# A pool of 46 slots in place of 45, and the modulation steps' unread products in a slot

## The chip, the core and the metric

The kernel runs on one core of one Trainium2 chip. The metric is the device time of one execution in microseconds (us). Engines are named as the profile names them: PE is TensorE (matmuls), PEld its loads of the stationary operand, DVE is VectorE, ACT is ScalarE, POOL is GpSimd, SP issues nearly all DMAs. SBUF is the on-chip memory of 128 partitions in which all tiles below lie, PSUM the accumulators of TensorE.

## What is computed

Two layers of a diffusion backbone on 640 tokens (512 latent, 128 context) of width 1024. A layer is an FFN, a mixer and a second FFN, each with a residual, a norm and a modulation of its own:

```
mod = silu(cond) @ ada_w + ada_b          # per layer: sh1, sc1, g1, sh2, sc2, g2, sh3, sc3, g3
h = rmsnorm(x, p['norm'][0]) * (1 + sc1) + sh1
x = x + 0.5 * g1 * swiglu(h, p['wg'][0], p['wu'][0], p['wd'][0])
h = rmsnorm(x, p['norm'][1]) * (1 + sc2) + sh2
x = x + g2 * mixer(h)                     # window means | attention | order-2 Hyena, then w_out
h = rmsnorm(x, p['norm'][2]) * (1 + sc3) + sh3
x = x + 0.5 * g3 * swiglu(h, p['wg'][1], p['wu'][1], p['wd'][1])
```

with `swiglu(h) = (silu(h @ wg) * (h @ wu)) @ wd` and an inner width of 2816. The context's attention keys and values are outputs too.

## The kernel before, in words

**Arithmetic.** Tokens are columns, features are partitions; `x` stays in SBUF as 8 chunks of 128 features by 640 tokens, worked on in two halves of 320 (`HT`). Each fp32 operand is split into a high and a low part (`hhi`, `hlo` for activations, `whi`, `wlo` for weights: ScalarE casts, L295, VectorE subtracts, L296), and three matmuls stand for one. Most gate and up products of an FFN go through `Seven`, a scheme that makes seven block products of eight.

**An FFN** (`ffn`, L684 and following) has 22 inner chunks in three parts of 8, 7 and 7. For each part it makes the inner chunks (`pr`, then its split `ahi`, `alo`) and then adds their part of the down projection to `x` for the 8 output chunks (`residual`, L566 to L572). In the last part the first three output chunks are made with weights loaded as they come; the last five (`DNSKEW`), the *tail*, have their weights kept in SBUF (`load_keep`, L312: tiles `kwh`, `kwl`) and are done half by half: all five for half 0, then all five for half 1, so that the next norm of half 0 can start while half 1 is multiplied. After each chunk `ssq_add` (L451) squares the new `x` on ScalarE (L453) and adds it to the sum on VectorE (L455), both into a slot `sq`. `Norm.stat` (L472) sums these over features with a matmul (`tot`, L477), makes `var` (L480) and `rs` on POOL; `scale` makes `dg` (L499), `apply` makes `y`, `hhi`, `hlo`.

**The pool of slots** (`sp`, L213) has `SLOTS` tiles of 640 fp32 numbers per partition under one tag. Nearly everything that lives longer than a moment takes one through `slot` or `slot3`: `hhi`, `hlo`, `pr`, `ahi`, `alo`, `y`, `sq`, `kwh`, `kwl`, the twisted inputs of `Seven`, the mixer's tables and spectra. A new tile has to wait until one of the pool's tiles is free.

**The modulation.** Three of the nine groups of layer 0 are made on TensorE in the prologue. The other 15 (of both layers) are made in steps on VectorE: a step multiplies a 128 by 1024 tile of `ada_w` (`araw`) by the conditioning vector and sums along the row into one column of `mods`; the instruction also writes the 1024 products, which nothing reads (`junk`, L408 to L411). A DMA of 512 KB (L401) serves two steps, and two `araw` tiles take turns. There are 240 steps, 80 each in the first FFN of layer 0, the second FFN of layer 0 and the first FFN of layer 1 (`PLAN`); none in the mixers or the last FFN. `ada_plan` spreads them over an FFN by weights (`ADAW`), and `ada_tick` issues those that are due: after each inner chunk (following `pack`), after each output chunk, and in the tail after each chunk of half 0. `issue_after` holds a step behind the last residual or `pr` product.

**What sets the order.** Each engine's instructions are put in order when the kernel is built: by their place in the program's text, by the priorities that `tc.high_priority` gives to weight loads and splits, and by when their inputs and tiles are free. TensorE's order is the text's. The order of the text in the tail matters here:

```
for d in range(DC - tail):                            # chunks 0, 1, 2
    if tail and d == DC - tail - 1:
        kept.append(load_keep(src(d + 1)))            # chunk 3's weights
    ...residual and ssq_add for both halves...
    ada_tick(last_w if end else down_w)               # L781
...
kept += [load_keep(src(d)) for d in ds_[len(kept):]]  # L786: chunks 4 to 7
nxt.kept = nxt.lead()                                 # first weights of the next stage
for half in range(2):
    for q, d in enumerate(ds_):
        residual(...); ssq_add(d, half)
        if half == 0: ada_tick(tail_w)                # L793
        if half == 1 and q == ST: nxt.stat(0)
```

Of the kernel before, what the change touches and what calls it, by code (L numbers as in the profile page):

```python
# [13 lines left out]
BF16 = mybir.dt.bfloat16  # L14
# [3 lines left out]
P = 128  # L18
# [14 lines left out]
PROT = 8  # L33
AG0 = (1, 0, 2)
MIXT = 70
SLOTS = 45
PF = 8
WB = 5
EXB = 7
# [144 lines left out]
def hybrid_kernel(ctx: ExitStack, tc: tile.TileContext, a, depth=2, fc=22):  # L184
# [27 lines left out]
    wp = ctx.enter_context(tc.tile_pool(name="wp", bufs=4))  # L212
    sp = ctx.enter_context(tc.tile_pool(name="sp", bufs=SLOTS))  # L213
    tp = ctx.enter_context(tc.tile_pool(name="tp", bufs=2))
# [8 lines left out]
    def nm(s):  # L223
        count[0] += 1
        return f"{s}{count[0]}"

    def slot(n=NCOL, dt=F32, name="s"):
        return sp.tile([P, n], dt, tag="s", name=nm(name))
# [7 lines left out]
    def tiny(n, name="t", bufs=4):  # L236
        return tp.tile([P, n], F32, tag=f"{name}{n}", bufs=bufs, name=nm(name))
# [4 lines left out]
    def mix(n=512, name="mx"):  # L242
        return acc(n, mx, name)
# [130 lines left out]
    def bias(l, g):  # L374
        return PR(l, "adab").rearrange("p (g s c r) -> p g s c r", g=9, s=2, c=4)[:, g]
# [21 lines left out]
    def ada_group(l, g):  # L397

        def load(n):
            raw = wp.tile([P, 1024], F32, tag="araw", bufs=ARAWB, name=nm("araw"))  # L400
            DMA.dma_start(out=raw, in_=a["adat"][l * 9 + g - len(AG0), n])  # L401
            ada_raw[l, g, n] = raw

        def step(n):
            raw = ada_raw[l, g, n // 2]
            i, r = n // 2, n % 2
            c, s = i // 2, i % 2
            junk = tp.tile([P, 1024], BF16, tag="junk", bufs=1, name=nm("junk"))  # L408
            with tc.issue_after(pace[0]) if pace else nullcontext():
                V.tensor_tensor_reduce(out=junk, in0=raw, in1=condb[:, r], scale=1.0, scalar=bias(l, g)[:, s, c, r:r + 1],  # L410
                                       op0=ALU.mult, op1=ALU.add, accum_out=mods[l][:, g, c, s, r:r + 1])  # L411
            if n == 2 * DC - 1:
                done.add((l, g))

        for n in range(2 * DC):
            ada_q.append(((lambda n=n: load(n // 2)) if n % 2 == 0 else None, lambda n=n: step(n)))
# [41 lines left out]
    class Norm:  # L458
# [13 lines left out]
        def stat(self, half):  # L472
            if self.key[::3] in done:
                self.affine()
            s = ssq[half]
            tot = mix(3, "tot")
            for t, o in enumerate((0, P, HT - P)):  # L477
                PE.matmul(out=tot[:, t:t + 1], lhsT=s[:, o:o + P], rhs=ones[:, 0:1], start=True, stop=True)
            var = tiny(3, "var")
            V.tensor_scalar(out=var, in0=tot, scalar1=1.0 / 1024.0, scalar2=EPS, op0=ALU.mult, op1=ALU.add)  # L480
            rs = tiny(3, "rs")
            G.tensor_tensor(out=rs, in0=var, in1=mhalf, op=ALU.pow)
            self.rs = rs
# [1327 lines left out]
```

## Time and profile before

| | us |
|---|---|
| median of three executions | 2406.22 |
| the three executions | 2406.14, 2406.22, 2408.6 |
| the profiled execution | 2408.28 |
| span in its trace | 2406.5 |
| PE busy | 2363.9 (98%) |
| PEld busy | 2240.9 (93%) |
| DVE busy | 1919.6 (80%) |
| ACT busy | 1094.1 (45%) |

The profiled execution's time is its span and 1.8 us around it. The busy share of an engine is an average over stages. In this kernel the first FFN of layer 0 reaches from about 100 to 545 us, its mixer to 825, its second FFN to 1258, and layer 1 follows the same pattern, its first FFN to 1695 and its mixer to 1973. PEclk in a table of windows is the granted clock of TensorE as a share of full speed. A matmul's record of 0.31 us overlaps the next; starts come 0.15 us apart when nothing is waited for. In a timeline, a row with xN stands for N instructions in a row, and the idle time before it stands in brackets with what ended it; a start that lies a little before the end of the instruction ahead is overlap.

### The profile page before, as it was taken

What the parts mean: (1) busy time and instruction counts of PE and PEld (TensorE: products, weight loads), DVE (VectorE), ACT (ScalarE), POOL (GpSimd) and SP (SyncE); (2) the same over time, 40 slices, a digit from 0 to 9 for tenths busy, and PEclk for the clock granted to TensorE, in tenths of its full rate; (3) what the DMA queues carried; (4) which work ended last, traced back from release to release, by engine and by line L of the source; (5) the groups of instructions that cost most, each with busy time, mean ns of one, the idle gap of its engine ahead of it and who ended that gap; (6) DMA issues with size and microseconds to landing.
All of it is one profiled execution on the core that took longest, in us unless ns stands there. A gap on an engine that the chain in (4) does not pass through costs nothing.

```text
span 2406.5 us, 41068 instructions
## 1 busy us (share of the span) xinstructions
PE 2363.9 (98%) x15576; PEld 2240.9 (93%) x15576; DVE 1919.6 (80%) x3885; ACT 1094.1 (45%) x2228; POOL 18.2 (1%) x46
## 2 busy tenths in 40 slices
PE   8999999999989999999999999999998999999999
PEld 3799999999877999999999999999987799999999
DVE  7888888996786798888989889898778678567583
ACT  4654352534345553453535435253434555335251
POOL 0000000000000000000000000000000000000000
PEclk9999999999989999999999999999999999999999
DMA  9434434353310235344343343534231022222222
GB/s 320 173 101 128 134 117 155 107 172 114 102 45 14 71 110 162 124 125 144 115 137 108 119 136 115 166 110 158 91 112 54 18 71 80 79 84 78 85 68 90
DMA packets 132646, 270.37 MB, mean 112 GB/s; under 512 B 15002, under 2 KB 24924, under 8 KB 132320
## 3 DMA queue, kind: packets, MB, share of 16 engines
q1 hardware_dynamic: 132448, 267.75, 34.8%
q8 instruction: 122, 2.00, 0.4%
q14 instruction: 76, 0.62, 0.1%
HBM read 259.56 MB, written 8.13 MB: 111 GB/s over the span
## 4 chain that ended last, share of the span: by engine, by line
PE 88%; DVE 6%; issue 2%; DMA 1%; ACT 1%; SPq 1%; POOL 0%; POOLq 0%; DVEq 0%; ACTq 0%
PE mm L205 74%; PE Z L205 5%; PE yt L205 1%; PE o L205 1%; PE pt L209 1%; DVE junk L410 1%; PE fk L205 1%; PE mx L205 1%; PE ada L205 1%; PE zf L205 1%; DVE kwl L296 0%; DMA kf<-store 0%; DVE wlo L296 0%; PE rsb L205 0%; DVE rp L1308 0%
## 5 line engine op out<-in xcount | busy, mean ns | idle before, releaser
L205 PE MATMUL mm<-hhi,whi 128*128 128x320 f32 x1440 | 448.4, 311 | 1.1 <-ACT u L1224 1.1
L295 ACT CAST whi<-raw 128x512 fp32r<-128x512 f32 (+1 forms) x394 | 238.7, 606 | 463.3 <-PE mm L205 423.0
L205 PE MATMUL mm<-hlo,whi 128*128 128x320 f32 x1440 | 446.3, 310 | 0.0
L205 PE MATMUL mm<-hhi,wlo 128*128 128x320 f32 x1440 | 446.0, 310 | 0.0
L205 PE MATMUL mm<-alo,whi 128*128 128x320 f32 x1198 | 370.8, 310 | 0.8 <-DVE alo L296 0.8
L205 PE MATMUL mm<-ahi,whi 128*128 128x320 f32 x1198 | 370.8, 310 | 0.0
L205 PE MATMUL mm<-ahi,wlo 128*128 128x320 f32 x1198 | 370.7, 309 | 0.0
L296 DVE TENSOR_TENSOR wlo<-raw,whi 128x512 fp32r<-128x512 f32 (+1 forms) x394 | 263.3, 671 | 75.7 <-ACT whi L295 71.3
L410 DVE CUSTOM_DVE_ANT_0 junk<-araw,condb,par 128x1024 bf16<-128x1024 f32 x240 | 307.4, 1281 | 2.1 <-DMA araw<-in_adat 0.8
L205 PEld LDWEIGHTS mm<-hhi,whi 128*128 128x128 f32 x1440 | 270.5, 188 | 5.9 <-ACT u L1224 2.8
L205 PEld LDWEIGHTS mm<-hlo,whi 128*128 128x128 f32 x1440 | 270.8, 188 | 1.9 <-issue 1.8
L205 PEld LDWEIGHTS mm<-hhi,wlo 128*128 128x128 f32 x1440 | 270.5, 188 | 1.4 <-issue 1.4
L205 PE MATMUL mm<-tlo,whi 128*128 128x320 f32 x864 | 267.4, 309 | 0.0
L205 PE MATMUL mm<-thi,whi 128*128 128x320 f32 x864 | 267.4, 309 | 0.0
L205 PE MATMUL mm<-thi,wlo 128*128 128x320 f32 x864 | 267.3, 309 | 0.0
L205 PEld LDWEIGHTS mm<-alo,whi 128*128 128x128 f32 x1198 | 225.0, 188 | 1.0 <-DVE alo L296 1.0
L205 PEld LDWEIGHTS mm<-ahi,whi 128*128 128x128 f32 x1198 | 225.0, 188 | 0.1
L205 PEld LDWEIGHTS mm<-ahi,wlo 128*128 128x128 f32 x1198 | 225.0, 188 | 0.0
L295 ACT CAST whi<-ex 128x512 fp32r<-128x512 f32 x216 | 134.2, 621 | 188.0 <-PE mm L205 175.6
L296 DVE TENSOR_TENSOR wlo<-ex,whi 128x512 fp32r<-128x512 f32 x216 | 149.2, 691 | 32.6 <-ACT whi L295 28.4
L295 ACT CAST whi<-ws 128x512 fp32r<-128x512 f32 x144 | 89.4, 621 | 162.2 <-PE mm L205 123.1
L205 PEld LDWEIGHTS mm<-thi,whi 128*128 128x128 f32 x864 | 162.3, 188 | 0.0
(263 smaller groups left out, 4704.2 us busy)
## 6 DMA issues: line engine op xcount, KB each, us to landing
araw<-in_adat SPq DMA_DIRECT2D x120, 512.0 KB, 3.6
raw<-in_wgu SPq DMA_DIRECT2D x208, 256.0 KB, 3.1
ex<-in_wgu SPq DMA_DIRECT2D x144, 256.0 KB, 2.7
raw<-in_wd SPq DMA_DIRECT2D x128, 256.0 KB, 2.7
raw<-in_win SPq DMA_DIRECT2D x56, 256.0 KB, 3.0
ar<-in_ada SPq DMA_DIRECT2D x48, 256.0 KB, 5.4
raw<-in_wd SPq DMA_DIRECT2D x64, 192.0 KB, 2.6
tab<-in_tfi SPq DMA_DIRECT2D x32, 256.0 KB, 3.9
```

Source lines behind the costliest of these rows:

```text
L205: cls.order(nc.tensor.matmul(**k))
L209: cls.order(nc.tensor.transpose(**k))
L295: S.copy(out=hi, in_=src)
L296: V.tensor_tensor(out=lo, in0=src, in1=hi.bitcast(F32), op=ALU.subtract)
L410: V.tensor_tensor_reduce(out=junk, in0=raw, in1=condb[:, r], scale=1.0, scalar=bias(l, g)[:, s, c, r:r + 1], op0=ALU.mult, op1=ALU.add, ac ...
```

## The change

The pool has one tile more. The products that nothing reads go to a slot of that pool instead of to a tile of their own (128 partitions by 1024 bf16 numbers, one buffer, from the pool `tp`). `var`, three numbers per partition, has two buffers in place of four. Nothing else is changed.

```diff
--- before.py
+++ after.py
@@ -33,7 +33,7 @@
 PROT = 8
 AG0 = (1, 0, 2)
 MIXT = 70
-SLOTS = 45
+SLOTS = 46
 PF = 8
 WB = 5
 EXB = 7
@@ -405,7 +405,7 @@
             raw = ada_raw[l, g, n // 2]
             i, r = n // 2, n % 2
             c, s = i // 2, i % 2
-            junk = tp.tile([P, 1024], BF16, tag="junk", bufs=1, name=nm("junk"))
+            junk = slot(1024, BF16, "junk")
             with tc.issue_after(pace[0]) if pace else nullcontext():
                 V.tensor_tensor_reduce(out=junk, in0=raw, in1=condb[:, r], scale=1.0, scalar=bias(l, g)[:, s, c, r:r + 1],
                                        op0=ALU.mult, op1=ALU.add, accum_out=mods[l][:, g, c, s, r:r + 1])
@@ -476,7 +476,7 @@
             tot = mix(3, "tot")
             for t, o in enumerate((0, P, HT - P)):
                 PE.matmul(out=tot[:, t:t + 1], lhsT=s[:, o:o + P], rhs=ones[:, 0:1], start=True, stop=True)
-            var = tiny(3, "var")
+            var = tiny(3, "var", 2)
             V.tensor_scalar(out=var, in0=tot, scalar1=1.0 / 1024.0, scalar2=EPS, op0=ALU.mult, op1=ALU.add)
             rs = tiny(3, "rs")
             G.tensor_tensor(out=rs, in0=var, in1=mhalf, op=ALU.pow)
```

## Rows read from the trace of the kernel before

**Rows 1.** Page, part 1: busy us (share of the span) x instructions, per engine
```profile
PE 2363.9 (98%) x15576; PEld 2240.9 (93%) x15576; DVE 1919.6 (80%) x3885; ACT 1094.1 (45%) x2228; POOL 18.2 (1%) x46
```

**Rows 2.** Windows by stage: length, busy sum, PE, PEld, DVE, ACT, POOL, PEclk, DMA share, GB/s
```profile
120.00:480.00 360.00, 360.00 (x2457) 360.00 (x2456) 309.73 (x553) 160.38 (x303) 1.07 (x3) 1.00 0.40 124
510.00:540.00 30.00, 28.93 (x198) 28.41 (x197) 27.82 (x61) 10.45 (x21) 0.85 (x1) 1.00 0.63 205
...
650.00:710.00 60.00, 50.14 (x277) 42.99 (x277) 49.44 (x129) 27.92 (x69) 0.56 (x8) 0.93 0.22 76
```

**Rows 3.** Waits of TensorE: us in total, times, longest us
```profile
PE yt L205 <- DVE wlo L296: 8.3, 2, 4.2
PE pt L209 <- DVE sc L1357: 7.6, 4, 3.6
...
PE tot L205 <- DVE sq L455: 1.0, 1, 1.0
```

**Rows 4.** Page, part 5: the modulation steps; busy us, mean ns | idle before
```profile
L410 DVE CUSTOM_DVE_ANT_0 junk<-araw,condb,par 128x1024 bf16<-128x1024 f32 x240 | 307.4, 1281 | 2.1 <-DMA araw<-in_adat 0.8
```

**Rows 5.** Timeline of VectorE, first FFN's tail: start, us, engine, line, op [idle <-releaser]
```profile
511.18 0.34 DVE L572 SCALAR_TENSOR_TENSOR x<-mm,g,x 128x128 f32<-128x128 f32 x1
511.43 1.28 DVE L410 CUSTOM_DVE_ANT_0 junk<-araw,condb,par 128x1024 bf16<-128x1024 f32 x1
...
512.63 1.16 DVE L296 TENSOR_TENSOR kwl<-raw,kwh 128x512 fp32r<-128x512 f32 x2
...
515.18 1.28 DVE L410 CUSTOM_DVE_ANT_0 junk<-araw,condb,par 128x1024 bf16<-128x1024 f32 x1
...
516.38 0.55 DVE L566 SCALAR_TENSOR_TENSOR x<-mm,g,x 128x320 f32<-128x320 f32 x1
516.85 1.28 DVE L410 CUSTOM_DVE_ANT_0 junk<-araw,condb,par 128x1024 bf16<-128x1024 f32 x1
...
519.12 1.28 DVE L410 CUSTOM_DVE_ANT_0 junk<-araw,condb,par 128x1024 bf16<-128x1024 f32 x1
...
521.86 1.28 DVE L410 CUSTOM_DVE_ANT_0 junk<-araw,condb,par 128x1024 bf16<-128x1024 f32 x1
...
526.34 1.28 DVE L410 CUSTOM_DVE_ANT_0 junk<-araw,condb,par 128x1024 bf16<-128x1024 f32 x1
...
528.61 0.69 DVE L296 TENSOR_TENSOR kwl<-raw,kwh 128x512 fp32r<-128x512 f32 x1
...
534.88 0.50 DVE L455 TENSOR_TENSOR sq<-sq,sq 128x320 f32<-128x320 f32 x1
```

**Rows 6.** Timeline of ScalarE, the same tail
```profile
524.02 2.69 ACT L295 CAST kwh<-raw 128x512 fp32r<-128x512 f32 x4 [4.64 <-DMA raw<-in_win]
526.61 0.47 ACT L453 ACTIVATE sq<-x 128x320 f32<-128x320 f32 x1
```

**Rows 7.** Timeline of TensorE, the same tail
```profile
512.97 0.31 PE L205 MATMUL mm<-alo,kwh 128*128 128x320 f32 x1
513.38 0.41 PE L205 MATMUL mm<-ahi,kwl 128*128 128x320 f32 x1
```

**Rows 8.** Timeline of SP's DMA queue, the same tail
```profile
508.89 4.18 SPq L401 DMA_DIRECT2D araw<-in_adat  x2
```

**Rows 9.** Page, part 6, DMA issues: count, KB each, us to landing
```profile
araw<-in_adat SPq DMA_DIRECT2D x120, 512.0 KB, 3.6
```

**Rows 10.** Timeline of VectorE, second FFN's tail
```profile
1235.60 1.28 DVE L410 CUSTOM_DVE_ANT_0 junk<-araw,condb,par 128x1024 bf16<-128x1024 f32 x1
```

**Rows 11.** Timeline of SP's DMA queue, first mixer
```profile
677.24 1.75 SPq L261 DMA_DIRECT2D tab<-in_tfi  x4
```

**Rows 12.** Windows, first mixer; columns as in rows 2
```profile
676.00:680.00 4.00, 0.00 (x0) 0.00 (x0) 4.00 (x13) 0.58 (x1) 0.00 (x0) 1.00 0.40 130
```

**Rows 13.** Windows, after a wait in the first mixer; columns as in rows 2
```profile
708.00:716.00 8.00, 6.62 (x17) 4.23 (x17) 8.00 (x20) 5.24 (x11) 0.00 (x0) 0.57 0.10 33
```

## The prediction, made before the changed kernel was run

> **What bounds the kernel now.** I read the page's busy times first: TensorE works for 2363.9 us of a span of 2406.5 and VectorE for 80% of it [rows 1]. An average hides the stages, so next come the windows by stage [rows 2]: the body of an FFN has TensorE busy for 360.00 us out of 360, the end of the first FFN (510 to 540) for 28.93 of 30, the middle of the first mixer for 50.14 of 60. Nothing that is taken off VectorE or a queue in an FFN's body can shorten the kernel; something that delays a matmul there lengthens it by its whole delay, for no idle time is there to absorb it. Third come TensorE's waits [rows 3]: the longest are two of the mixers (8.3 us in two waits, 7.6 in four), and one at the FFN's end, 1.0 us for the sums of squares, `sq`. So the change is judged at two places: the mixers, where TensorE waits, and wherever a modulation step stands in front of something TensorE needs.
>
> **What the change alters.** The work is the same: 240 steps of 1281 ns, 307.4 us of VectorE [rows 4], the same loads, the same matmuls. Three things differ. A step's product has a slot of the common pool in place of a tile of its own; the pool is one slot larger; `var` has two buffers in place of four.
>
> *The order of the slots.* What matters is how slots are given out, and the trace shows it at the first FFN's end. There, `x` for one chunk was written at 516.38 in 0.55 us [rows 5], ScalarE sat idle for 4.64 us until 524.02, waiting for a weight's load, cast four pieces (`kwh`), and only then, at 526.61, squared that `x` [rows 6]. The only reason I find for a ready instruction to stand behind casts whose data had not come is the pool: `sq`, `kwh` and `kwl` are slots, and in the text of `ffn` the kept weights of the next stage (`nxt.lead()`) are taken before the loop over halves that takes those `sq`. So slots are granted in the order of the program's text: a later taker waits until the earlier ones have theirs, even with slots free. Before, `junk` was outside this line and its steps ran in whatever gap VectorE had. After, they stand in the line, in the place where `ada_tick` calls them.
>
> *In the bodies of the FFNs* (some 200 of the 240 steps) a step is called right after `pack` has taken `ahi` and `alo`, and the next takers are the next `pr`, some microseconds later. The step will go behind `alo` in place of just ahead of it. I cost this at nothing: TensorE is 100% busy on matmuls queued from tiles already there [rows 2], and the step waits for no one there. If that cover were gone, a delay of one step, 1.2 us, would be the price, at each of some 20 chunks per FFN; I keep it out of the range because the next `pr` is further off than a step is long.
>
> *The tails* (the last five output chunks of three FFNs: the first, the second, the third; the last FFN has neither steps nor a tail) are where the line binds. Here `ada_tick` after chunk 2 issues three steps, and right behind them in the text stand the kept weights of chunks 4 to 7 and of the next stage. In the trace VectorE ran the first of the three at 511.43, then `kwl` of chunk 4 at 512.63, and the other two at 515.18 and 516.85 [rows 5]. TensorE's first matmul on that `kwl` began at 513.38, 0.41 us after the one ahead of it [rows 7], in a stretch where one follows another every 0.15 us: there is no slack, it already waited for `kwl`. After the change the slot of `kwl` comes behind all three products, and `issue_after` holds the steps behind the residual at 511.18, so two further steps go ahead of `kwl`. From step to next instruction is 1.20 us (511.43 to 512.63): 2 x 1.20 = **2.4 us** later, and TensorE stands for as long. Their weights (`araw`) are there: the load issued at 508.89 [rows 8] takes 3.6 us [rows 9], so 512.5, when the second step would start. Bounds: 0 if `kwl` still slips in ahead; 2.9 if an `sq` add of 0.5 us (as the one at 534.88) also goes ahead. I take 2.4, as every row for it is there.
>
> *Second, in the same tail:* the six steps called in the loop over half 0 stand behind the last `kwl` of the next stage. Before, three of them (519.12, 521.86, 526.34) ran ahead of that `kwl` of 528.61, partly while VectorE had nothing else [rows 5]. After, they can't. From that `kwl`'s end, 529.2, to the end of the last `sq` add for half 0, 535.4 (started at 534.88), VectorE is full, with three steps in it; TensorE already waits 1.0 us there for `sq` [rows 3]. After: the `kwl` of the next stage comes 2.4 later with its loads (their `raw` buffers are freed by the `kwl` delayed above), less 1.2 for the step at 526.34 that is no longer ahead of it: 530.4. Then 6.2 us as before, plus three steps of 1.2, less one (the step of the last chunk stands behind its `sq` in the text): 8.6, so 539.0 in place of 535.4, 3.6 later. TensorE comes there 2.4 later, so 1.2 more is waited: **3.6 us for this tail in all**. Bounds: 2.4, if VectorE's gaps take the steps; 4.8, if all three go ahead of the last `sq`.
>
> The third tail repeats these rows. In the second the modulation queue runs dry: its last step is at 1235.60 [rows 10], two in the loop in place of six, so I take 2.4 alone. Sum of the tails: 3.6 + 2.4 + 3.6 = 9.6 us (0 to 4.8 + 2.9 + 4.8 = 12.5).
>
> *The 46th slot* can help where a taker waits for a slot to be freed. I find that at one place in each mixer: four table loads issued one after another over 1.75 us at 677.24, just when VectorE's products release `kf` [rows 11]. One slot more lets the last go at the time of the one ahead: 1.75 / 4 = 0.44 us per mixer, 0.9 us for two. But TensorE's wait there ends with VectorE (`wlo`) [rows 3], and VectorE is busy for 4.00 us of the 4.00 from 676 to 680 [rows 12]. So between 0 and 0.9; I take 0.9.
>
> *`var` with two buffers* costs nothing: POOL reads it at once, and the next but one `var` is of another norm. Were a wait to come, it would be among those of `tot`, 1.0 us in all [rows 3].
>
> *The granted clock.* After a mixer's wait of 3.6 us the clock was granted at 0.57 over 708 to 716 [rows 13], so for most of it TensorE had the lower of its levels, 1.2 in place of 2.4 GHz: (1 - 0.57) x 8 = 3.4 us lost. After the wait of 1.0 at the tail it stayed at 1.00 [rows 2]. A stall of 2.4 lies between these; I take no loss, and keep 3 x 3.4 = 10.2 for the range.
>
> **The sum.** The profiled execution took 2408.28 us (span 2406.5 and 1.8 around it), 2.1 above the median 2406.22, and the largest part of that difference I cannot place in the trace; I add the change to the median: 2406.2 + 9.6 - 0.9 = **2415** us.
>
> **The rivals.**
> - *The 46th slot serves as the products' own tile.* If a ready `kwl` or `sq` need not wait for a step's slot, all stays where it is and the change is one of names. For it: one slot is added and one taker comes. Against it: the `sq` that waited almost 10 us behind four casts [rows 5, 6]. Time: 2405 to 2406.
> - *Faster: the mixers lacked a slot.* If the table loads were the true cause of TensorE's longest waits and one more slot lets them go early, up to 8.3 us goes [rows 3], 2398, and 2391 with the clock that is not lost after it (2 x 3.4). It decides only if the tables, not VectorE, come last; VectorE's 4.00 of 4.00 [rows 12] speaks against it. The Trainium skill, "Perfetto Trace Analysis", section "Optimization Strategy", has this as a rule: the same gap repeated on the engine that should be saturated can mean that there is no room in SBUF for the next tile. By that rule the added slot would give the mixers' time back; the trace has the same gap in both mixers, as the rule says, but shows a busy VectorE as its releaser.
> - *Slower by more: the clock falls.* If a stall of 2.4 us is enough, each of the three tails loses up to 3.4 more: 2415 + 10 = 2425.
>
> **How the numbers follow.** Forecast (three tails, no clock loss) 0.42; the clock falls in some 0.20; no change 0.28; faster 0.10, where I also count what a reordering may gain that I don't see. About 0.2% (4.8 us) is what a measurement of this kernel can tell from no change. So faster 0.10, same 0.28, slower 0.62. The range starts at 2404, which takes in the case without change, and ends at 2406.2 + 12.5 + 10.2 - 0.9 = 2428; left out are the faster cases and a worse clock. The likeliest case alone is 2411 to 2419.
>
> **What would show it.** Right: in the tails three steps stand back to back ahead of `kwl` of chunk 4 (at 511.4 in the first), TensorE has a new wait for `kwl` of 2 to 3 us in each, no step runs between there and the last `kwl` of the next stage, and the wait of `tot` for `sq` grows to about 2 us in the first and third. FFN bodies stay at 100%, mixers within 0.5 us. Wrong: steps still interleave with `kwl` in the tails (then it is the first rival), or the waits of `yt` shrink by more than 1 us (the second), or TensorE gaps turn up in the FFN bodies, which I cost at nothing.

## The result and the profile after

| | before | after |
|---|---|---|
| median, us (4 executions each) | 2406.48 (2406.14 to 2408.6) | 2430.77 (2426.78 to 2433.13) |
| ratio, with its 95% interval | | 1.0092 (1.0075 to 1.0109) |
| profiled execution, us | 2408.28 | 2426.78 |
| span, us | 2406.5 | 2425.0 |

By the medians the kernel became 24.3 us slower; the ratio, taken over all executions, is 0.9%. The forecast was slower, 2415 us, with a range to 2428: the direction is right, the size is not, and the median lies 2.8 us above the range. The execution with the trace is the shortest of the four after; against the trace of before it is 2426.78 - 2408.28 = 18.5 us longer, and those 18.5 us can be placed, to a tenth or two.

The page of the changed kernel, part 1, answers to rows 1: TensorE's records are a little longer in sum, the other engines' are within 0.4% of what they were.

```profile
PE 2376.0 (98%) x15576; PEld 2246.6 (93%) x15576; DVE 1912.7 (79%) x3885; ACT 1090.4 (45%) x2228; POOL 18.5 (1%) x46
```

TensorE's waits after, in the columns of rows 3. The three waits for `kwl` are new; those for `yt` are shorter and have another releaser; the one for `tot` grew from 1.0 to 1.6; `pt` is as before.

```profile
PE mm L205 <- DVE kwl L296: 8.7, 3, 3.0
PE pt L209 <- DVE sc L1357: 7.6, 4, 3.6
PE yt L205 <- DMA tab<-in_tfi: 6.9, 4, 2.9
...
PE tot L205 <- DVE sq L455: 1.6, 1, 1.6
```

The windows after, in the columns of rows 2. In the body TensorE still counts as busy all the time (360.00 of 360), but it did 2444 matmuls where before it did 2457 [rows 2], and its weight loads are no longer back to back: PEld 358.18. The tail went from 28.93 busy us to 25.57.

```profile
120.00:480.00 360.00, 360.00 (x2444) 358.18 (x2443) 306.04 (x549) 157.38 (x300) 1.26 (x3) 1.00 0.39 124
...
510.00:540.00 30.00, 25.57 (x173) 25.05 (x173) 25.11 (x47) 9.65 (x19) 0.00 (x0) 0.99 0.60 202
```

**Where the 18.5 us lie.** Both traces have 15576 matmuls. Paired by their order on TensorE, the distance from the start of each to the start of the next can be subtracted and summed by stretch (times of before):

| stretch | after less before, us |
|---|---|
| prologue, 0 to 120 | -0.9 |
| first, second, third FFN body (120 to 500, 820 to 1215, 1270 to 1640) | +1.9, +2.3, +1.8 |
| first, second, third tail (500 to 560, 1215 to 1270, 1640 to 1720) | +5.5, +4.4, +4.7 |
| first, second mixer (560 to 820, 1720 to 1970) | -2.8, +1.8 |
| last FFN, 1970 to the end | 0.0 |

The tails have 14.6 of it, the bodies 6.0, and the mixers, where the 46th slot should help, give back 1.0; the prologue is 0.9 shorter.

**The first tail after.** VectorE's timeline, to be held against rows 5. All three steps after chunk 2 stand ahead of `kwl` of chunk 4, with the `sq` add between the first and the second; no step runs between there and the last `kwl` of the next stage, though VectorE sits idle for 3.14 us; then all six of the loop follow, the first at 530.47.

```profile
512.18 1.28 DVE L410 CUSTOM_DVE_ANT_0 junk<-araw,condb,par 128x1024 bf16<-128x1024 f32 x1
513.39 0.08 DVE L410 DVE_READ_ACCUMULATOR2_ANT mod<- 128x1 f32 x1
513.39 0.48 DVE L455 TENSOR_TENSOR sq<-sq,sq 128x320 f32<-128x320 f32 x1
513.79 1.28 DVE L410 CUSTOM_DVE_ANT_0 junk<-araw,condb,par 128x1024 bf16<-128x1024 f32 x1
...
515.00 1.28 DVE L410 CUSTOM_DVE_ANT_0 junk<-araw,condb,par 128x1024 bf16<-128x1024 f32 x1
...
516.21 1.16 DVE L296 TENSOR_TENSOR kwl<-raw,kwh 128x512 fp32r<-128x512 f32 x2
...
527.12 1.38 DVE L296 TENSOR_TENSOR kwl<-raw,kwh 128x512 fp32r<-128x512 f32 x2 [3.14 <-ACT kwh L295]
...
530.47 1.28 DVE L410 CUSTOM_DVE_ANT_0 junk<-araw,condb,par 128x1024 bf16<-128x1024 f32 x1
```

TensorE's timeline in the same tail answers to rows 7. The first matmul on that `kwl` starts 3.15 us after the one ahead of it in place of 0.41. The same matmul of the second and third tail follows below; there the distance grew from 0.41 to 3.32 and 3.15, so the three tails have 8.4 us more of it.

```profile
513.80 0.31 PE L205 MATMUL mm<-alo,kwh 128*128 128x320 f32 x1
516.95 0.41 PE L205 MATMUL mm<-ahi,kwl 128*128 128x320 f32 x1 [2.84 <-DVE kwl L296]
...
1235.81 0.49 PE L205 MATMUL mm<-ahi,kwl 128*128 128x320 f32 x1 [3.01 <-DVE kwl L296]
...
1679.80 0.64 PE L205 MATMUL mm<-ahi,kwl 128*128 128x320 f32 x1 [2.84 <-DVE kwl L296]
```

**The clock in the tails.** Windows after, one in each tail (columns of rows 2). The granted clock is 0.66 over 5 us in each, so part of each stretch ran at the lower level, 1.2 GHz: (1 - 0.66) x 5 = 1.7 us lost per tail, 5.1 in all. Before, it was 1.00 over the whole first tail [rows 2]. In the first tail the drop comes only after the wait for `tot` at 539; in the other two it follows the one for `kwl` at once.

```profile
539.00:544.00 5.00, 4.96 (x25) 4.96 (x26) 4.22 (x14) 1.42 (x3) 0.85 (x1) 0.66 0.39 134
1235.00:1240.00 5.00, 4.19 (x18) 4.19 (x19) 2.75 (x7) 0.00 (x0) 0.00 (x0) 0.66 0.68 243
1679.00:1684.00 5.00, 4.20 (x18) 4.20 (x19) 2.74 (x7) 0.56 (x1) 0.00 (x0) 0.66 0.78 268
```

So the tails' 14.6 are: 8.4 more of waiting for `kwl`, 5.1 of clock, 0.6 more at `tot`; together 14.1.

**The bodies.** What was costed at nothing has a price. In each of the three bodies 18 to 20 distances from one matmul to the next grew, nearly all by 0.06 to 0.15 us and one by 0.41, mostly two or three close together; where the rows were read, a weight load had waited. The group of weight loads that shows most of it, before and then after (the groups by line; the last part is the idle time before them):

```profile
L205 PEld LDWEIGHTS mm<-thi,whi 128*128 128x128 f32 x864 | 162.3, 188 | 0.0
```

```profile
L205 PEld LDWEIGHTS mm<-thi,whi 128*128 128x128 f32 x864 | 162.0, 188 | 3.9 <-ACT rc L616 2.0
```

One of these places in the timeline of TensorE and of its weight loads after, in the second part of the first FFN. Three matmuls of one product (`thi`, `tlo`) have come in between two of another (`hhi`, `hlo`), and the next weight load waits 0.24 us for VectorE's `rc` (a product read out of PSUM). Before, twelve matmuls on `hhi` and `hlo` follow one another here, with 0.15 us from each to the next.

```profile
293.11 0.31 PE L205 MATMUL mm<-thi,whi 128*128 128x320 f32 x1
293.26 0.31 PE L205 MATMUL mm<-tlo,whi 128*128 128x320 f32 x1
293.40 0.31 PE L205 MATMUL mm<-thi,wlo 128*128 128x320 f32 x1
293.69 0.41 PE L205 MATMUL mm<-hhi,whi 128*128 128x320 f32 x1
```

```profile
293.69 0.19 PEld L205 LDWEIGHTS mm<-hhi,whi 128*128 128x128 f32 x1 [0.24 <-DVE rc L621]
```

This corrects a sentence ahead of the prediction: TensorE's order is not simply the text's. The matmuls of two products of `Seven` are interleaved, and a step at another place moves how. It is not one place alone: compared matmul by matmul, by the names of their tiles, each of the three bodies differs from before at 194 places, in 8 stretches, and 54 of the 56 distances that grew lie within eight matmuls of such a place. Why the order comes out this way (presumably by when inputs are expected) no run shows.

### The profile page after: what moved, and what is told of

The parts are those of the page before. It is cut to its first block, busy times and chain, and to the rows that moved or that the text cites. A ratio compares the mean times of both kernels' runs of the same rounds, so it can differ in the third digit from the quotient of the medians.

```text
span 2425.0 us, 41010 instructions
## 1 busy us (share of the span) xinstructions
PE 2376.0 (98%) x15576; PEld 2246.6 (93%) x15576; DVE 1912.7 (79%) x3885; ACT 1090.4 (45%) x2228; POOL 18.5 (1%) x46
## 4 chain that ended last, share of the span: by engine, by line
PE 69%; DVE 4%; issue 2%; DMA 1%; ACT 1%; POOL 0%; SPq 0%; POOLq 0%; DVEq 0%; ACTq 0%
PE mm L205 59%; PE Z L205 4%; PE yt L205 1%; PE o L205 1%; PE pt L209 1%; PE zf L205 1%; DVE junk L410 1%; DMA araw<-in_adat 0%; DVE wlo L296 0%; DMA raw<-in_wd 0%; DVE kwl L296 0%; PE rsb L205 0%; PE nps L205 0%; DMA tab<-in_tfi 0%; DVE sc L1154 0%
## 5 line engine op out<-in xcount | busy, mean ns | idle before, releaser
L205 PEld LDWEIGHTS mm<-tlo,whi 128*128 128x128 f32 x864 | 162.2, 188 | 0.0
```

What stands on the lines that cost most here:

```text
L205: cls.order(nc.tensor.matmul(**k))
```

## The experiments

Each was timed beside executions of the kernel before on the same chip, whose median was 2407.2 us for the first four runs, 2410.5 for the next four, then 2410.2 and 2407.8. On some chips these spread by 10 us and more, so the ratios and the traces decide, not the bare times. A ratio is taken over all executions and need not be that of the two medians.

### The line without the 46th slot, and the 46th slot without the line

First, the products in a slot of a pool of 45, `var` untouched:

```diff
-            junk = tp.tile([P, 1024], BF16, tag="junk", bufs=1, name=nm("junk"))
+            junk = slot(1024, BF16, "junk")
```

> The pool keeps 45 slots and the products go to a slot; `var` keeps four buffers. If the loss comes from the place of the steps in the line of slots (the theory), the three tails keep their stalls for `kwl` (about 2.9 us each) and the bodies their small waits, and the mixers' waits for `yt` are again 4.2 us each: about 2.5 us more than the changed kernel, some 2429 to 2433 us. If the loss comes from the 46th slot (the rival: one more slot shifts the order of everything), the time is the old one, 2406 us within 0.2%.

Measured: 2429.38 us, ratio 1.0090 (1.0075 to 1.0105). Its waits:

```profile
PE mm L205 <- DVE kwl L296: 8.5, 3, 2.8
PE yt L205 <- DVE wlo L296: 8.3, 2, 4.2
...
PE tot L205 <- DVE sq L455: 2.1, 1, 2.1
```

The whole loss is there with 45 slots, and the waits for `yt` are the old ones. The 46th slot has no part in the loss that can be seen; the 2.5 us that the longer waits for `yt` were expected to add are less than the two intervals can tell. The wait for `tot` is 2.1 us here, where the changed kernel has 1.6.

Second, the changed kernel with one slot taken once and held for all products:

```diff
-            junk = slot(1024, BF16, "junk")
+            junk = spare[0]
...
+    spare = [slot(1024, BF16, "junk")]
```

> 46 slots, but one is taken once and held for the products of all steps, so that no step stands in the line of slots and 45 are left for the rest. Theory: the time of before, 2406 us within 0.2%, tails without a stall for `kwl`. Rival (the slot's size or place in SBUF, or the two buffers of `var`, cost something): 2415 us or more.

Measured: 2405.82 us, ratio 0.9997 (0.9986 to 1.0007), no wait for `kwl` in the list. The size and place of the tile, the pool's length and the two buffers of `var` cost nothing that the interval of 0.1% to either side can tell; what costs is that each step asks for a slot in its turn. One of its two waits for `yt` was 2.9 us, though only 45 slots were left to the rest, which speaks against the next run's reason for it.

Third, one slot held per FFN, so that the mixers have all 46:

```diff
-            junk = slot(1024, BF16, "junk")
+            if hold[0] is None:
+                hold[0] = slot(1024, BF16, "junk")
+            junk = hold[0]
...
+    hold = [None]
...
         g = None
+        hold[0] = None
         hs = cur.hs
```

> 46 slots; the products of all steps of one FFN share one slot that is taken at its first step, so that the mixers have 46 and the FFNs 45 and a tile of their own. Theory: tails and bodies as before, and the mixers' waits for `yt` as in the changed kernel (2.9 in place of 4.2 us each): 2403 to 2404 us. Rival (the shorter waits for `yt` come from the changed arrival of the work, not from the slot): 2406 us.

Measured: 2407.41 us, ratio 0.9995 (0.9983 to 1.0007). TensorE's waits for `yt`:

```profile
PE yt L205 <- DMA tab<-in_tfi: 7.3, 4, 2.9
```

The two long waits are 2.9 us, as in the changed kernel, but two more for the tables follow, so the sum is 7.3 where it was 8.3 + 0.5. The waits shrink as the theory says, and the time does not show it: 1.5 us are 0.06%, less than this interval can tell from nothing.

### Which steps cost what

The next runs have 45 slots and the products' own tile again, except for the steps of one place. A variable `zone` says where a step is called; `junk` is a slot there and the old tile elsewhere, and the tile costs no wait, since only VectorE writes it:

```diff
-            junk = tp.tile([P, 1024], BF16, tag="junk", bufs=1, name=nm("junk"))
+            junk = slot(1024, BF16, "junk") if zone[0] == "body" else tp.tile([P, 1024], BF16, tag="junk", bufs=1, name=nm("junk"))
...
+                zone[:] = ["turn" if tail and d == DC - tail - 1 else "body", 0]
                 ada_tick(last_w if end else down_w)
+                zone[0] = "body"
...
+                            zone[0] = "loop"
                             ada_tick(tail_w)
+                            zone[0] = "body"
```

**The bodies** (`zone[0] == "body"`):

> 45 slots and a tile of their own for the products as before, but the steps of the bodies (all but those after chunk 2 and in the loop over half 0 of a tail) write to a slot. Theory: the order of the matmuls in `Seven` changes as in the changed kernel and each of the three bodies loses about 2 us in waits of 0.1 to 0.4: 2411 to 2413 us, no stall for `kwl` in the tails. Rival (the drift in the bodies follows from what the tails did to the order, or is chance): 2406 us within 0.2%.

Measured: 2413.95 us, ratio 1.0029 (1.0014 to 1.0044), no wait for `kwl`. The waits of the weight loads have the two rows that the changed kernel has and the kernel before has not:

```profile
PEld mm L205 <- ACT rc L617: 2.0, 12, 0.2
PEld mm L205 <- DVE rc L622: 1.4, 6, 0.2
```

Paired with before, its bodies are 1.8, 2.7 and 1.8 us longer: the drift is the steps' own doing, without any tail. TensorE's order differs from before at as many places as in the changed kernel, 194 in each body.

**The three steps after chunk 2** (`zone[0] == "turn"`):

> 45 slots and a tile of their own for the products, except for the three steps after chunk 2 of each tail, which write to a slot. Theory: the stall for `kwl` of chunk 4 alone, 2.8 us in each tail, and about 1.7 us of half clock behind it: 3 x 4.5 = 13.5, some 2420 us. Rival (the stall needs the steps of the loop in the line too): no wait for `kwl` above 0.5 us, 2406 to 2408 us.

Measured: 2423.36 us, ratio 1.0061 (1.0041 to 1.0081). Three stalls, 2.9, 3.0 and 3.5 us:

```profile
PE mm L205 <- DVE kwl L296: 9.4, 3, 3.5
```

Its tails are 4.2, 4.4 and 4.7 us longer and its bodies not at all (sums of 0.0). These nine steps of 240 are two thirds of the loss.

**The steps of the loop over half 0** (`zone[0] == "loop"`):

> 45 slots and a tile of their own, except for the steps in the loop over half 0 of each tail, which write to a slot. By the prediction's second term they crowd VectorE ahead of the last `sq` of half 0, so that the wait of `tot` grows by 1 to 2 us in the first and third tail: 2408 to 2410 us. Rival (VectorE makes room, as in the changed kernel, whose waits for `tot` grew by 0.6 us only): 2406 us within 0.2%, waits for `tot` of 2 us at most.

Measured: 2410.08 us, ratio 1.0006 (0.9993 to 1.0018), and the longest wait for `tot` is 1.3 us:

```profile
PE tot L205 <- DVE sq L456: 1.3, 1, 1.3
...
PE mm L205 <- DVE hlo L534: 1.0, 2, 0.5
```

The prediction's second term is not there in its own form: six steps move behind the last `kwl`, and TensorE waits 0.3 us longer for `tot` in one tail, where 1.2 in each of two was forecast. In this execution the first tail was 3.5 us longer all the same: the clock behind that wait was 0.66 over 533 to 538, 1.7 us lost, and the waits for `hlo` of the next norm (second row) are new. The ratio does not show this loss, but its interval reaches to 0.18%, 4.3 us, so it does not rule it out either.

The three parts add up, as far as their intervals of 0.12 to 0.2% to either side can tell: 0.29 + 0.61 + 0.06 = 0.96%, against 0.90 for all of them in the run with 45 slots and 0.92 for the change.

**Two of the three steps** after chunk 2 (`zone[0] == "turn"` for the first two alone):

> As the run with the three steps after chunk 2 in slots, but only the first two of them: one step of 1.2 us is taken away from ahead of `kwl`. Theory: stalls for `kwl` of 2.8 - 1.2 = 1.6 us in each tail. If half clock follows such a stall too, 3 x (1.6 + 1.7) = 10 us, 2416 us; if not, 3 x 1.6 less the 0.3 that TensorE waited before, 2410 us. Rival (the delay is not the steps' own time but a wait for a free slot): the same 2.8 us as with three.

Measured: 2412.76 us, ratio 1.0017 (1.0002 to 1.0031). The first matmuls on `kwl` of chunk 4 in its three tails, from the timeline of TensorE:

```profile
510.93 0.41 PE L205 MATMUL mm<-ahi,kwl 128*128 128x320 f32 x1 [1.71 <-DVE kwl L296]
...
1225.16 0.41 PE L205 MATMUL mm<-ahi,kwl 128*128 128x320 f32 x1 [1.71 <-DVE kwl L296]
...
1665.27 0.41 PE L205 MATMUL mm<-ahi,kwl 128*128 128x320 f32 x1 [2.35 <-DVE kwl L296]
```

Windows behind two of these stalls, in the first and the third tail (columns of rows 2):

```profile
510.00:516.00 6.00, 5.07 (x34) 5.07 (x35) 6.00 (x13) 1.04 (x2) 0.00 (x0) 1.00 0.82 253
...
1666.00:1671.00 5.00, 5.00 (x25) 5.00 (x25) 5.00 (x10) 1.03 (x2) 0.00 (x0) 0.66 0.83 268
```

One step less takes 2.91 - 1.71 = 1.20 us off the stall in the first tail, exactly the 1.20 from one step to the next instruction in rows 5: the stall is VectorE's order, not a search for a free slot. And after the stall of 1.71 the clock stayed at 1.00, after the one of 2.35 it was 0.66 over 5 us. Paired with before, the three tails of this trace are 1.7, 1.6 and 3.6 us longer, 6.9 in place of the 13.4 with three steps: half, with one step less in three, because two of the three tails lose no clock. The ratios fell by more, from 0.61 (0.41 to 0.81) to 0.17% (0.02 to 0.31); their intervals allow a half.

### The bodies' steps ahead of `pack`

```diff
-                acts.append(w.pack())
-                ada_tick(up_w)
+                ada_tick(up_w)
+                acts.append(w.pack())
```

on top of the run of the bodies:

> As the run whose bodies' steps write to a slot, with the step issued ahead of `pack` in place of behind it, so that its slot is granted before `ahi` and `alo`, as its place in VectorE's order was before. Theory: the order of the matmuls in the bodies is the old one, the 18 to 20 small waits per body are gone: 2406 us within 0.2%. Rival (a step in a slot disturbs the bodies wherever it is called): 2411 to 2414 us.

Measured: 2409.68 us, ratio 1.0001 (0.9987 to 1.0015). The group of weight loads that had 3.9 us of idle time:

```profile
L205 PEld LDWEIGHTS mm<-thi,whi 128*128 128x128 f32 x864 | 162.2, 188 | 0.1
```

With its slot granted ahead of `ahi` and `alo` the step costs the bodies next to nothing (their sums are 0.4, 0.5 and 0.4 us), and TensorE's order in the three bodies is that of before at every place. So the place behind `alo` is what the bodies paid for, and the changed order of the matmuls comes and goes with it.

### Versions

The changed kernel with the step ahead of `pack` as above, and no step after the output chunks of an FFN's last part, so that more are issued in the bodies:

```diff
-ADAW = (1.0, 1.25, 2.0, 0.75)
+ADAW = (1.0, 1.25, 0.0, 0.0)
```

> The changed kernel (46 slots, all products in slots), with the step issued ahead of `pack` in the bodies and no steps in the last three and the tail's five output chunks (the weights of `ADAW` for them are 0, so the bodies have more). Theory: both places where a step stands ahead of a split that TensorE needs are gone, so the whole loss is gone: 2404 to 2409 us, no stall for `kwl`. Rival (VectorE, 86% busy in the bodies before, becomes the bound there with some 18% more steps): waits in the bodies, 2412 us or more.

Measured: 2405.70 us, ratio 0.9992 (0.9981 to 1.0002). The loss is gone with the products still in slots, as it should be if the two places were the cause. This run does two things at once, though: emptying the tails gives a gain of its own, 0.9978 without any slot (below). Against that run the slots may still cost something like 0.1%, which is not shown, for the two intervals overlap. The trace points that way: TensorE waits 2.2 us for `alo` in two waits, 0.4 in the run without slots, and the first body is 1.7 us longer than before, there 0.3.

The same weights on the version that holds one slot per FFN:

> The version whose FFNs each hold one slot of 46 for the products, with no steps in the last eight output chunks of an FFN. If the steps in the tail cost the 1.0 us wait for `sq` there, it is gone: 2405 to 2406 us; the same 2406 us within 0.2% otherwise. Rival as above: 2412 us or more if the denser bodies make TensorE wait.

Measured: 2402.65 us, ratio 0.9970 (0.9959 to 0.9980). And on the kernel before, with 45 slots and the products' own tile, nothing changed but `ADAW`:

> The kernel before (45 slots, products in a tile of their own), with the steps kept out of the last eight output chunks of each FFN and nothing else changed. It divides the gain of the version with a held slot: if it comes from the tails alone (no step between the `kwl` and `sq` there), this gives 2403 to 2405 us; if from the 46th slot in the mixers (waits for `yt` of 2.9 in place of 4.1 us), this stays at the time of before within 0.2% and shows waits of 4.1 us.

Measured: 2403.06 us, ratio 0.9978 (0.9967 to 0.9989). On the same chip the held version once more:

> The same kernel as the run it repeats, on the same chip as the one above: again 0.2 to 0.4% below before, 2402 to 2404 us, if the gain is the kernel's; within 0.2% of before if it was the chip's.

Measured: 2402.57 us, ratio 0.9982 (0.9970 to 0.9993). Both beat the kernel before and the changed one. The windows of the kernel before with the new weights, in the body and in the first tail: VectorE does 325.11 us of the 360 in place of 309.73 [rows 2], TensorE does not notice, and the tail is full.

```profile
120.00:480.00 360.00, 360.00 (x2457) 360.00 (x2456) 325.11 (x583) 159.52 (x300) 1.91 (x3) 1.00 0.43 136
```

```profile
510.00:540.00 30.00, 30.00 (x209) 29.96 (x208) 20.96 (x47) 12.85 (x26) 0.85 (x1) 1.00 0.32 102
```

The waits for `yt` are 4.1 and 4.3 us with 45 slots here and 2.9 with 46 held:

```profile
PE yt L205 <- DMA tab<-in_tfi: 4.5, 2, 4.3
PE yt L205 <- DVE wlo L296: 4.1, 1, 4.1
```

```profile
PE yt L205 <- DMA tab<-in_tfi: 6.2, 3, 2.9
```

The intervals of the two versions overlap, so the gain belongs to the steps taken out of the tails; the slot adds nothing that can be told from nothing. Paired with before, the three tails of the version without a slot are 1.7, 0.4 and 1.2 us shorter, 3.3 of the 5.2 us by which its trace is shorter.

## Why the prediction was wrong

**The order of the slots: right.** The mechanism that was read from one `sq` waiting behind four casts holds. The changed kernel's steps stand where the text calls them, and the first rival (the 46th slot serves as the products' tile) is what one gets only by holding that slot (0.9997).

**The first term, the stall for `kwl`: right, its size at the upper bound.** Forecast 2.4 us in each of three tails, upper bound 2.9 with an `sq` add among the steps; measured as waits 2.84, 3.01 and 2.84, with that add at 513.39. Against before TensorE comes to that matmul 2.74, 2.91 and 2.74 us later, together 8.4 us in place of 7.2.

**The second term, the loop's steps: VectorE right, TensorE wrong.** 1.2 us more at `tot` were forecast for the first and for the third tail. In the first, VectorE did what was worked out: the last `kwl` ended at 530.1 (forecast 530.4) and the last `sq` add of half 0 at 539.0 (forecast 539.0; the add at 538.49, from VectorE's timeline). That it agrees to the tenth is in part luck: this tail's first step began at 512.18 in place of 511.43, 0.75 us late through the body, which the forecast did not have. But TensorE came there 3.0 us later than before (free at 537.45 in place of 534.47), not 2.4: the stall was longer, the tail began later, and four matmuls that had stood ahead of `tot` came behind it. So the wait grew by 0.6. For the third tail the forecast took the first to be repeated; rows 3, which it cites, list a wait for `tot` once among all tails, so there was slack in the third, and no wait came up there after either. The term was 0.6 us in place of 2.4 in this trace (1.1 in the run with 45 slots), and the run of the loop alone puts it at 0.06% (-0.07 to 0.18), which does not exclude the 0.10% that was forecast. So the two terms together came out at 9.0 us where 9.6 were forecast, the first 1.2 above and the second 1.8 below: that sum is close by luck.

**The clock: the wrong choice between two cases.** The rival "the clock falls" had a chance of 0.20; it happened in all three tails, though in the first not behind the stall that was meant. Its price was overrated: 3.4 us per tail, from a window in a mixer; measured 1.7. A stall of 2.4 lay between one of 1.0 without and one of 3.6 with the loss, and I took none, although 2.4 already lies nearer to the 3.6 (1.2 away) than to the 1.0 (1.4 away).

**The bodies at nothing: the step that failed.** "The step waits for no one there" is not what decides, and "TensorE is 100% busy on matmuls queued from tiles already there" is where it goes wrong. The busy share of a window cannot show slack: matmul records overlap, and 360.00 of 360 stands in both traces, with 13 matmuls fewer in the second. What the step's new place moves is not a tile that TensorE lacks but the interleaving of two products on TensorE (194 places in each body), and that opens 18 to 20 small waits per body, 6.0 us in all. The prediction's first paragraph had the right warning, that whatever delays a matmul there costs its whole delay; the zero went against it. I named 1.2 us at each of some 20 chunks as the price if the cover failed, and left it out of the range; a third of the traced loss was there.

**The mixers: the forecast size, and the rule.** 0.9 us were forecast; the changed kernel's trace has 1.0 less. But a trace of one execution can't carry that: the granted clock differs from execution to execution (22 executions of the kernel before on one chip had 0.988 to 0.995 as their mean), and with it the clock over the mixers from trace to trace. Windows of 75 us over the middle of both mixers, for the kernel before, the changed one, and the run with the line and 45 slots:

```profile
645.00:720.00 75.00, 65.14 (x334) 52.48 (x333) 61.74 (x155) 33.11 (x81) 0.56 (x8) 0.91 0.26 88
1795.00:1870.00 75.00, 65.24 (x352) 53.61 (x351) 62.81 (x157) 34.88 (x89) 0.56 (x8) 0.95 0.26 89
```

```profile
650.00:725.00 75.00, 65.65 (x354) 53.94 (x353) 63.13 (x158) 34.61 (x89) 0.56 (x8) 0.95 0.26 89
1812.00:1887.00 75.00, 67.19 (x340) 54.59 (x339) 61.91 (x156) 33.57 (x83) 0.56 (x8) 0.89 0.27 89
```

```profile
650.00:725.00 75.00, 65.98 (x340) 54.17 (x339) 62.09 (x154) 32.98 (x79) 0.56 (x8) 0.89 0.26 87
1815.00:1890.00 75.00, 65.82 (x336) 53.60 (x335) 62.03 (x154) 33.09 (x79) 0.56 (x8) 0.89 0.27 89
```

Lost to the clock: (0.09 + 0.05) x 75 = 10.5 us before, (0.05 + 0.11) x 75 = 12.0 after, (0.11 + 0.11) x 75 = 16.5 in the third, whose profiled execution took 2430.73 us against 2426.78. So two traces can differ by several us in the mixers alone. The medians differ by 24.3 and the traced executions by 18.5. Of the remaining 5.8 us, 1.8 are by how much the trace of before is longer than its median, and 4.0 by how much that of after is shorter. What makes the other executions longer stays open: they left no trace, and the clock does not tell them apart, for the shortest of the four after (2426.78) and the longest (2433.13) both had a mean of 0.991.

The rule of the Trainium skill's "Perfetto Trace Analysis" (section "Optimization Strategy"), that a repeated gap can mean missing room for the next tile, comes out half right here: with 46 slots the repeated gap shrank from about 4.1 to 2.9 us in four kernels (the changed one, both that hold a slot per FFN, and the one without steps in the tails), and once with 45. The time did not follow visibly: where only that was changed, the ratio is 0.9995 (0.9983 to 1.0007), and the sum of the waits had fallen by only 1.5 us, because further waits for the tables came behind the shorter ones. My reason against it, that VectorE sets the end of that wait, was too strong, for the wait did shrink.

**The chances.** Slower had 0.62, and slower it was. The likeliest case had the tails right and missed two terms of its own size, the bodies (6.0) and the clock (5.1); the range's upper end, 2428, was built from the clock at twice its price and the bodies at nothing, and those two errors nearly cancelled. What was placed in the traces, 18.5 us, would lie inside the range; the median lies 2.8 us above it by the 5.8 that stay open, but with the bodies' 6.0 in its upper end the range would have held it.

## What to carry to other kernels

A pool with one tag is also a queue: moving a short-lived buffer into it makes its owner wait its turn in the text, and makes later takers wait for the owner, even when nothing waits for a free tile: three such steps ahead of `kwl` made TensorE stand for 2.8 to 3.5 us in each tail, two for 1.7 to 2.4, and with one tile held for good these waits were gone. Before a buffer is moved into such a pool, list who takes a tile right behind it, and where one of them feeds the engine that sets the time, keep the buffer apart or hold one tile for good. Work that can be done at any time is best kept out of the stretches where the engine that sets the time waits for splits made by the engine that does it: taking the steps out of the tails was worth 0.2% (0.1 to 0.3) by itself, without any slot.

## What the runs showed of the hardware

The clock did not answer to a stall's length alone. After stalls for `kwl` of 2.35 us (two steps, third tail), 2.84 and 3.01 us (the changed kernel, third and second tail) and 2.91, 2.98 and 3.48 us (three steps, all tails) it was 0.66 over 5 us, which costs 1.7 us more; after stalls of 1.71 us (two steps, first and second tail) it stayed at 1.00. But in the changed kernel's first tail it also stayed at 1.00 after 2.84 us, and fell over 20 us later, behind a wait of 1.6 us for `tot`. The window over that first stall (columns of rows 2):

```profile
507.00:522.00 15.00, 12.16 (x83) 11.90 (x82) 13.30 (x26) 4.29 (x9) 0.00 (x0) 1.00 0.61 197
```

A window in which TensorE counts as busy for 360.00 of 360 us can still have lost 1.9 us; the count of its matmuls (2457 and 2444, before and after) and the busy time of its weight loads (360.00 and 358.18) show it.
